# A two-layer hybrid encoder on one core: TensorE's small steps pinned in emission order, and two attention stages that hand over twice as often

## The chip, the cores and the metric

One core of one Trainium2 chip runs the whole program. The time is device microseconds from launch to end; the kernel before was run three times (2702.85, 2710.77 and 2712.8 us, median 2710.77 us), and once more with the profiler. The engines are named as in the profile: PE is TensorE's matmuls, PEld its weight loads, DVE is VectorE, ACT ScalarE, POOL GpSimd, SP the engine that issues the DMAs.

## The reference

The model is an encoder of two layers on a sequence of 1024 tokens with 1024 features, in float32. What matters of it:

```python
h = rms_norm(x, norm1_g[l])
proj = h @ w_in[l]                       # columns for four head groups
y_a = mla_mixer(...)    # A: 4 heads, full softmax over 1024 keys, latent q, k, v
y_b = diff_mixer(...)   # B: 4 heads, each softmax(q0 k0) - lam * softmax(q1 k1), then rms_norm of the head
y_c = swa_mixer(...)    # C: 4 heads, a band of +-128 keys and a sink
y_d = na_mixer(...)     # D: 4 heads, a 2-D neighbourhood with a learnt bias
mix = concatenate([rms_norm(y_a), y_b, rms_norm(y_c), rms_norm(y_d)])
x = x + mix @ w_out[l]
x = x + square(relu(rms_norm(x, norm2_g[l]) @ w_up[l])) @ w_down[l]
```

After the second layer comes a last rms_norm.

## The kernel before

Everything is kept transposed, features on the partitions and tokens along the free axis. A float32 product is made of three passes over operands split into a rounded high part and a low remainder: high by high, high by low, low by high (`passes`, L222 to L224). A pass is one matmul of 128x512. Splitting a weight block takes an ACT copy (L196) and a subtraction on POOL (L190).

A layer runs through these stages. First, projections of the columns for B, with every bank of PSUM. Then four attention stages, B, D, C and A, each as the *main* stream of a helper `weave`, with projections as its *fill*: in B the fill is three latent projections for A and the six for D; in D the four for C and A's products from the latent (`mm<-latp`); in C and A the early part of the output projection (`mm<-mix...`). Then the rest of the output projection, and the MLP, whose TensorE order is written out by hand.

In B and A (`dense`) the main stream goes by groups of 256 queries: for each 128 queries scores on PE (`sb<-stack`, two matmuls of 128x512 for each softmax in B, six in A), the minimum on DVE (L812), the exponential on ACT (L815); B makes two softmaxes for each 128 queries and combines them on ACT (L898) and POOL. The tiles of the group before are meanwhile transposed on PE (`tr<-ident,p`), split on ACT (`pth<-tr`) and DVE (`ptl<-tr`), and multiplied with the values (`pv<-pth`, `pv<-ptl`). In D and C (`banded`) it goes by 128 keys, and the scores are 128x256 or 128x384.

Beside main and fill there are *tails*: a queue of small chains that finish what a head has begun. A chain of denominators (`denominators`) takes the reciprocal on DVE, transposes the 128x8 column on PE (`mm<-ident,rz`), copies it, stores it to DRAM and loads it back spread over the partitions. A chain of norms (`sub_norm`, `mix_group`) goes on: multiply on POOL, square on ACT, sum by a matmul with ones (`mm<-pairs,rz` or `mm<-ones,sq`), reciprocal root, transpose (`mm<-ident,rs_r`), store, spread, multiply, split (`mixh`, `mixl`). `tick` takes one step of the first chain.

`weave` takes one step of main at a time, and after each step `every` ticks (the numbers `EV`) and `ratio` steps of fill. What it fixes is the emission order. The order in which each engine gets its instructions is then found by a scheduler, which knows the dependencies, the tiles' buffers and a priority: the place in emission order, moved ahead by `lead` instructions for main (40 in B, 50 in D, 0 in C and A). Buffers bind it too: the projections, the transposed columns and the sums of the norms all take turns on two PSUM banks, `mm`. Every engine then works through its own instructions strictly in that order.

Of the kernel before, what the change touches and what calls it, by code (L numbers as in the profile page):

```python
# [144 lines left out]
    return t.rearrange("f h s -> (f h) s")  # L145


class Trunk:
    def __init__(self, ctx, tc, d, out):
        self.ctx, self.tc, self.nc, self.d, self.out = ctx, tc, tc.nc, d, out  # L150
        self.ahead, self.tails = 4, deque()
        pool = lambda **k: ctx.enter_context(tc.tile_pool(**k))
        self.const = pool(name="const", bufs=1)
        self.xp = pool(name="xp", bufs=8)
        self.big = pool(name="big", bufs=16)
        self.wp = pool(name="wp", bufs=3)
        self.cp = pool(name="cols", bufs=2)
        self.dram = pool(name="dram", bufs=1, space=bass.MemoryType.DRAM)
# [222 lines left out]
    def attention(self, l):  # L381
# [33 lines left out]
        def proj_c():  # L415
            tabs = self.table("64", rb, nc.gpsimd)
            for t in range(2):
                yield from one(T_CQ2[t], xs, self.ev_rope(tabs, qc[:, t]))
            yield from one(T_CK, xs, self.ev_rope(tabs, kc))
            yield from one(T_CV, xs, self.ev_plain(rb, self.to_values(vc)))  # L420
# [3 lines left out]
        with ExitStack() as stack, ExitStack() as att:  # L424
            self.ap = att.enter_context(sbuf("att"))
            with self.banks(mm=2, tr=2, sb=3, pv=1):
                with sbuf("proj", "right") as self.pp:
# [20 lines left out]
                    for t in range(2):  # L448
# [6 lines left out]
                        if t == 0:  # L455
# [5 lines left out]
                    self.weave(chain.from_iterable(self.attn_b(l, t, qb, kb, vb, y["b"]) for t in range(2)),  # L461
                               fill, self.RB, self.LB, every=self.EV[0])
                    self.tails.append(self.mix_b(mix, y["b"], self.gsub[:, l:l + 1]))
                    fill = chain(proj_c(), self.latent_up(l, lat, rows, qa, ka, va))
                    self.weave(self.attn_d(l, qd, kd, vd, y["d"]), fill, self.RD, self.LD, every=self.EV[1])
                gout = lambda n: self.gout[n][:, l]
# [5 lines left out]
                def groups_bd():  # L472

                    for m in range(self.EARLY):
                        x = wo.tile([P, S], F, tag="sum", bufs=self.EARLY, name="sum")
                        self.load(x, saved[m])
                        sums.append(x)
                    while None in mix[:4]:
                        yield True
                    for m, x in enumerate(sums):  # L480
                        ws = self.weights(w_out[m, 0])
                        for n in range(2):
                            ps = self.mm_ps()
                            self.product(ps, ws, mix[:4], n)
                            sl = slice(n * 512, n * 512 + 512)
                            self.tt(x[:, sl], ps, x[:, sl], ALU.add)
                            yield True

                fill = groups_bd()
                self.weave(self.attn_c(l, qc, kc, vc, y["c"]), fill, self.RC, end=False, every=self.EV[2])  # L490
                self.tails.append(self.mix_group(mix, 4, y["c"], gout("swa")))
                self.weave(self.attn_a(l, qa, ka, krd, va, y["a"]), fill, self.RA, self.LA, every=self.EV[3])
                self.tails.append(self.mix_group(mix, 6, y["a"], gout("mla"), nc.vector))
# [43 lines left out]
                        self.product(ps, ws, mix[4:], n)  # L537
                        add(x, ps, partial, n)

    EV = (.5, .5, .7, 1)  # L540
    EARLY, RC, RA, LA = 4, (8, 1), (3, 1), 0
    WAVES = [(T_BQ[t], T_BK[t], T_BV[t]) for t in range(2)]
    NP, RB, RD, LB, LD = 6, (7, 8), (3, 2), 40, 50

    def weave(self, main, fill=iter(()), ratio=(1, 0), lead=0, end=True, every=1):


        due, steps = ratio[1] if lead else 0, 0
        while True:
            with self.tc.high_priority(offset=lead):  # L550
                if next(main, None) is None:
                    break
            steps += every
            while steps >= 1:
                steps -= 1
                self.tick()
            due += ratio[1]
            while due >= ratio[0]:
                due -= ratio[0]
                next(fill, None)  # L560
        if end:
            for _ in fill:
                pass
# [207 lines left out]
        yield  # L771


    def tick(self):
        while self.tails:
            if next(self.tails[0], self) is not self:
                return
            self.tails.popleft()

    def drain(self):  # L780
        while self.tails:
            self.tick()
# [35 lines left out]
    def dense(self, heads):  # L818

        nc = self.nc
        ready = []

        def product(job, j, h, lo):
            probs, g, v, y, half, done = job
            if g % 2 == 0 and j == 0:
                self.pv = self.bank("pv")
            out = self.pv[:, (g % 2) * 256:(g % 2) * 256 + 256]  # L830
            for k in range(2):
                kt = j * 2 + k
                sl = slice(k * 256, k * 256 + 256)
                nc.tensor.matmul(out, v[:, kt], h[:, sl], start=kt == 0, stop=False)  # L834
                nc.tensor.matmul(out, v[:, kt], lo[:, sl], start=False, stop=kt == 7)  # L835
            if j == 3:
                if g % 2:
                    self.pv_out(self.pv, y, half, g // 2)
                if g == 3:
                    done()  # L840

        def step(job, j):
            t = self.bank("tr")
            for k in range(2):
                for i, p in enumerate(job[0]):
                    nc.tensor.transpose(t[:, k * 256 + i * P:k * 256 + (i + 1) * P],  # L846
                                        p[:, (j * 2 + k) * P:(j * 2 + k + 1) * P], self.ident)
            h, lo = self.transposed(512)
            self.split(h, lo, t)
            ready.append((job, j, h, lo))  # L850
            if len(ready) > 1:
                product(*ready.pop(0))

        job = None
        for head in heads:
            tile_probs, *rest = head()
            for g in range(4):
                probs = []
                for i in range(2):
                    probs.append(tile_probs(g * 2 + i))  # L860
                    if job:
                        step(job, 2 * i)
                        step(job, 2 * i + 1)
                job = (probs, g, *rest)
                yield True
        for j in range(4):
            step(job, j)
        product(*ready.pop(0))
        yield True
# [629 lines left out]
```

## Time and profile before

| what | value |
| --- | --- |
| median of three runs | 2710.77 us (2702.85 to 2712.8) |
| profiled execution, its span | 2709.95 us, 2707.9 us |
| PE busy, share of the span | 2549.6 us, 94% |
| DVE, ACT, POOL busy | 1943.0, 1439.8, 1130.9 us |
| layer 1: B, then D, then C | 83 to 330, to 406, to 480 us |
| layer 1: A, then the output projection | 480 to 635, to 699 us |
| layer 1: MLP | 699 to 1345 us |
| layer 2: B, then D, then C | 1420 to 1669, to 1749, to 1820 us |

The boundaries are the starts of the first scores of a stage on PE. The second layer repeats the first. A page's PE row counts a matmul from its start to a modelled end, so matmuls that follow each other closely overlap; how far apart they start is read from the timeline.

### The profile page before, as it was taken

Reading aid. Unit: us, or ns where it says so; the run is one execution under the profiler, and the core shown is the slowest. Engines: PE = TensorE matmul, PEld = TensorE weight load, DVE = VectorE, ACT = ScalarE, POOL = GpSimd, SP = SyncE. Lnnn points to the kernel's source line nnn. Section 1 sums busy time; section 2 is a strip of 40 time slices with the busy share of each in tenths; the row PEclk is TensorE's granted clock in tenths of the full one; section 3 lists DMA queues with packets and bytes.
Section 4 is the critical chain, followed back from the end, with each engine's and each line's share of the span. In section 5 each row is a group of like instructions: output and inputs, shape, how many; then the busy total and the mean of one; then the engine's idle time right before and its main releaser. Section 6 shows DMA issues by size and latency. Waiting matters only on the chain.

```text
span 2707.9 us, 37502 instructions
## 1 busy us (share of the span) xinstructions
PE 2549.6 (94%) x12296; PEld 2112.5 (78%) x12296; DVE 1943.0 (72%) x3379; ACT 1439.8 (53%) x2601; POOL 1130.9 (42%) x754
## 2 busy tenths in 40 slices
PE   8989988999899998999999999889998999999997
PEld 6778876787778887888877788668876788878886
DVE  6777866774966668887567777677749666688775
ACT  4667756664534444444436776566635344444444
POOL 2555642201345554545434656321013455544442
PEclk9989988999999999999998899899999999999998
DMA  5534597222144457444244446962221444664431
GB/s 175 169 107 129 158 287 239 82 89 63 46 144 148 153 170 267 143 142 141 95 139 134 121 113 183 295 202 69 71 71 52 154 153 152 221 221 146 136 105 63
DMA packets 186931, 389.19 MB, mean 144 GB/s; under 512 B 23712, under 2 KB 26736, under 8 KB 186736
## 3 DMA queue, kind: packets, MB, share of 16 engines
q1 hardware_dynamic: 172912, 361.62, 43.2%
q10 hardware_dynamic: 13824, 25.17, 2.7%
q8 instruction: 97, 1.59, 0.2%
q14 instruction: 98, 0.80, 0.1%
HBM read 263.29 MB, written 123.41 MB: 143 GB/s over the span
## 4 chain that ended last, share of the span: by engine, by line
PE 73%; DVE 12%; DMA 6%; ACT 4%; issue 3%; POOL 1%; SPq 0%; DVEq 0%; ACTq 0%; POOLq 0%
PE u L222 8%; PE u L224 8%; PE u L223 8%; PE mm L222 5%; PE mm L223 5%; PE mm L224 5%; PE p L222 5%; PE p L223 5%; PE p L224 5%; PE sb L810 3%; PE tr L846 3%; DVE p L812 2%; DVE part L190 2%; PE pv L835 2%; PE pv L834 2%
## 5 line engine op out<-in xcount | busy, mean ns | idle before, releaser
L190 POOL TENSOR_TENSOR wl<-raw,wh 128x512 fp32r<-128x512 f32 x448 | 632.8, 1413 | 704.8 <-ACT wh L196 691.0
L196 ACT ACTIVATE wh<-raw 128x512 fp32r<-128x512 f32 x448 | 281.5, 629 | 576.2 <-PE u L223 310.9
L190 POOL TENSOR_TENSOR wl<-ws,wh 128x512 fp32r<-128x512 f32 (+1 forms) x112 | 147.3, 1316 | 461.0 <-ACT wh L196 436.1
L222 PE MATMUL u<-far,wh 128*128 128x512 f32 x768 | 301.8, 393 | 11.4 <-ACT ev L1242 8.3
L224 PE MATMUL u<-far,wl 128*128 128x512 f32 x768 | 300.6, 391 | 2.2 <-POOL wl L190 2.2
L190 DVE TENSOR_TENSOR raw<-raw 128x512 f32<-128x512 f32 x256 | 223.1, 877 | 109.1 <-POOL wl L190 55.6
L223 PE MATMUL u<-far,wh 128*128 128x512 f32 x768 | 300.6, 391 | 0.0
L190 DVE TENSOR_TENSOR ptl<-tr,pth 128x512 fp32r<-128x512 f32 (+2 forms) x384 | 238.3, 629 | 68.5 <-ACT pth L196 66.8
L815 ACT ACTIVATE p<-p,nm 128x1024 f32<-128x1024 f32 x192 | 220.2, 1147 | 92.3 <-DVE nm L812 91.6
L196 ACT ACTIVATE pth<-tr 128x512 fp32r<-128x512 f32 (+2 forms) x384 | 205.2, 546 | 108.5 <-PE tr L846 64.9
L222 PE MATMUL p<-far,wh 128*128 128x512 f32 x640 | 252.9, 395 | 7.5 <-DVE ev L190 7.5
L224 PE MATMUL p<-far,wl 128*128 128x512 f32 x640 | 251.5, 393 | 1.5 <-POOL wl L190 1.5
L223 PE MATMUL p<-far,wh 128*128 128x512 f32 x640 | 252.2, 394 | 0.0
L810 PE MATMUL sb<-stack 96*128 96x512 f32 x640 | 217.5, 422 | 22.1 <-DVE nm L812 21.4
L190 DVE TENSOR_TENSOR far<-act,far 128x512 fp32r<-128x512 f32 x224 | 207.3, 955 | 14.7 <-ACT far L196 14.7
L190 POOL TENSOR_TENSOR p<-p 128x1024 f32<-128x1024 f32 x64 | 154.0, 2411 | 129.6 <-ACT p L898 121.3
L222 PEld LDWEIGHTS u<-far,wh 128*128 128x128 f32 x768 | 145.3, 189 | 43.5 <-ACT ev L1242 9.1
L222 PE MATMUL mm<-xh,wh 128*128 128x512 f32 x416 | 170.9, 411 | 0.8 <-DVE part L190 0.3
L224 PEld LDWEIGHTS u<-far,wl 128*128 128x128 f32 x768 | 145.2, 189 | 33.5 <-POOL wl L190 3.0
L812 DVE CUSTOM_DVE_ANT_0 p<-sb,zero,nm 128x512 f32<-128x512 f32 x192 | 142.4, 743 | 37.7 <-PE sb L810 34.6
L223 PEld LDWEIGHTS u<-far,wh 128*128 128x128 f32 x768 | 145.4, 189 | 30.0
L223 PE MATMUL mm<-xl,wh 128*128 128x512 f32 x416 | 167.7, 403 | 0.0
(245 smaller groups left out, 6110.1 us busy)
## 6 DMA issues: line engine op xcount, KB each, us to landing
act<-acts SPq DMA_DIRECT2D x224, 256.0 KB
raw<-in_w_up SPq DMA_DIRECT2D x128, 256.0 KB
acts<-ev SPq DMA_DIRECT2D x128, 256.0 KB
raw<-in_w_down SPq DMA_DIRECT2D x128, 256.0 KB
acts<-ev ACTq DMA_DIRECT2D x96, 256.0 KB
ws<-in_w_in SPq DMA_DIRECT2D x76, 256.0 KB
rz<-drows SPq DMA_DIRECT2D x40, 256.0 KB
stack<-kd SPq DMA_DIRECT2D x32, 256.0 KB
```

Source lines behind the costliest of these rows:

```text
L190: (eng or self.nc.vector).tensor_tensor(out=out, in0=a, in1=b, op=op)
L196: nc.scalar.activation(hi, src, AF.Copy)
L222: mm(ps, w[0], x[0][:, sl], start=start, stop=False)
L223: mm(ps, w[0], x[1][:, sl], start=False, stop=False)
L224: mm(ps, w[1], x[0][:, sl], start=False, stop=stop)
L810: self.nc.tensor.matmul(ps, q[:, qt * P:(qt + 1) * P], k[:, sl], start=i == 0, stop=i == len(passes) - 1)
L812: self.nc.vector.tensor_tensor_reduce(out=p[:, sl], in0=ps, in1=self.zero[:, 0:1].bitcast(F).broadcast_to([P, 512]), scale=-scale, scalar= ...
L815: self.nc.scalar.activation(p, p, AF.Exp, bias=nm[:, 1:2], scale=-1.0, accum_out=z)
L834: nc.tensor.matmul(out, v[:, kt], h[:, sl], start=kt == 0, stop=False)
L835: nc.tensor.matmul(out, v[:, kt], lo[:, sl], start=False, stop=kt == 7)
L846: nc.tensor.transpose(t[:, k * 256 + i * P:k * 256 + (i + 1) * P], p[:, (j * 2 + k) * P:(j * 2 + k + 1) * P], self.ident)
```

## The change

A wrapper `Kept` is put around TensorE. While a tick of `weave` runs, each TensorE instruction that it emits is tied behind the TensorE instruction emitted just before it. The scheduler may no longer move it ahead of that one; it may still move other work past it. Only TensorE's steps are tied: the DVE, ACT, POOL and DMA steps of the same chains are placed as before.

`dense` now yields after the first 128 queries of a group as well as after the second. B and A so have twice as many steps, and their ratios of fill are halved to match: `RB` from (7, 8) to (7, 4), `RA` from (3, 1) to (6, 1). `EV` for B goes from .5 to .3, so that B has 0.6 ticks where it had 0.5; for A it stays 1, so that A has two ticks where it had one. No instruction is added or removed.

```diff
+class Kept:
+    def __init__(self, trunk, engine):
+        self.trunk, self.engine = trunk, engine
+
+    def __getattr__(self, name):
+        f = getattr(self.engine, name)
+
+        def emit(*args, **kw):
+            ins = f(*args, **kw)
+            if self.trunk.kept and name != "dma_start":
+                self.trunk.tc.keep_in_program_order(ins)
+            return ins
+
+        return emit
+
 class Trunk:
+    KEPT = ("tensor",)
...
-        self.ctx, self.tc, self.nc, self.d, self.out = ctx, tc, tc.nc, d, out
+        self.ctx, self.tc, self.d, self.out = ctx, tc, d, out
+        engines = {e: getattr(tc.nc, e) for e in ("tensor", "vector", "scalar", "gpsimd", "sync")}
+        self.kept = False
+        self.nc = SimpleNamespace(**{n: Kept(self, e) if n in self.KEPT else e for n, e in engines.items()})
...
-    EV = (.5, .5, .7, 1)
-    EARLY, RC, RA, LA = 4, (8, 1), (3, 1), 0
+    EV = (.3, .5, .7, 1)
+    EARLY, RC, RA, LA = 4, (8, 1), (6, 1), 0
...
-    NP, RB, RD, LB, LD = 6, (7, 8), (3, 2), 40, 50
+    NP, RB, RD, LB, LD = 6, (7, 4), (3, 2), 40, 50
...
-                self.tick()
+                self.tick(True)
...
-    def tick(self):
+    def tick(self, kept=False):
+        self.kept = kept
         while self.tails:
             if next(self.tails[0], self) is not self:
-                return
+                break
             self.tails.popleft()
+        self.kept = False
...
                     if job:
                         step(job, 2 * i)
                         step(job, 2 * i + 1)
+                    if i == 0:
+                        yield True
```

What it does to the order is seen in three places. In the changed kernel every TensorE instruction is issued by the wrapper's line, so all of them read L158; ScalarE's lines are moved by 23 or more.

First, TensorE in stage B of the first layer, at the transposed denominators of the second head (`mm<-ident,rz`). `tr`, `pv` and `sb` are attention, `mm<-xh` and `mm<-xl` a projection. Before:

```order
L835 MATMUL pv<-ptl,v 128x256
L834 MATMUL pv<-pth,v 128x256
L810 MATMUL sb<-stack 128x512
L835 MATMUL pv<-ptl,v 128x256
L834 MATMUL pv<-pth,v 128x256
L835 MATMUL pv<-ptl,v 128x256
L846 MATMUL tr<-ident,p 128x128 x4
L810 MATMUL sb<-stack 128x512
L846 MATMUL tr<-ident,p 128x128 x4
L273 MATMUL mm<-ident,rz 8x128
L222 MATMUL mm<-xh_164,wh 128x512
```

Now:

```order
L158 MATMUL sb<-stack 128x512 x2
L158 MATMUL pv<-ptl,v 128x256
L158 MATMUL pv<-pth,v 128x256
L158 MATMUL pv<-ptl,v 128x256
L158 MATMUL pv<-pth,v 128x256
L158 MATMUL tr<-ident,p 128x128
L158 MATMUL sb<-stack 128x512 x2
L158 MATMUL pv<-ptl,v 128x256
L158 MATMUL pv<-pth,v 128x256
L158 MATMUL pv<-ptl,v 128x256
L158 MATMUL mm<-ident,rz 8x128
L158 MATMUL mm<-xh_164,wh 128x512
```

In both a projection begins right behind the transposes. Before, 66 of B's 128 scores and 240 projection matmuls stand ahead of them; now 79 scores and 192 projection matmuls, and the 89 instructions just ahead (16 of them scores) hold no projection at all.

Second, TensorE in D of the first layer, at the transposed denominators of B's third head (before, they come among B's last scores). Before, among the scores of D's first head:

```order
L223 MATMUL mm<-xl_193,wh 128x512
L982 MATMUL sb<-stack 128x384 x2
L224 MATMUL mm<-xh_192,wl 128x512
L846 MATMUL tr<-ident,p 128x128 x6
L834 MATMUL pv<-pth,v 128x256
L982 MATMUL sb<-stack 128x384 x2
L835 MATMUL pv<-ptl,v 128x256
L834 MATMUL pv<-pth,v 128x256
L835 MATMUL pv<-ptl,v 128x256
L982 MATMUL sb<-stack 128x384 x2
```

Now, at the end of the scores of D's second head:

```order
L158 MATMUL sb<-stack 128x384 x2
L158 MATMUL sb<-stack 128x256 x2
L158 MATMUL pv<-ptl,v 128x384
L158 MATMUL mm<-ident,rz 8x128
L158 MATMUL mm<-xh_164,wh 128x512
L158 MATMUL mm<-xl_165,wh 128x512
L158 MATMUL mm<-xh_164,wl 128x512
L158 MATMUL mm<-xh_168,wh 128x512
L158 MATMUL mm<-xl_169,wh 128x512
L158 MATMUL mm<-xh_168,wl 128x512
```

Now 72 projection matmuls stand between these scores and the next. Over the layer, 554 of the 624 projection matmuls stood ahead of D's first score, and now 414 do; ahead of D's second head it was 600, now 432, ahead of the third 624, now 552. Counted over B's TensorE order of the first layer, 18 of the 128 scores lay in stretches of 28 or more instructions with no projection among them, and now 52 do. In A, 96 early products of the output projection were done, now 84.

Third, ScalarE in stage B, at the square of the pair's output (`rz<-y`), which needs these same denominators after their way through DRAM and a multiplication on POOL. Before:

```order
L815 ACTIVATE p,z_2093<-p,nm 128x1024
L196 ACTIVATE pth<-tr 128x512
L196 ACTIVATE wh<-ws 128x512
L898 ACTIVATE p<-p,cb 128x1024
L916 ACTIVATE rz<-y 128x1024
L815 ACTIVATE p,z_2092<-p,nm 128x1024
L196 ACTIVATE wh<-ws 128x512
```

Now:

```order
L840 ACTIVATE p,z_2065<-p,nm 128x1024
L925 ACTIVATE p<-p,cb 128x1024
L219 ACTIVATE pth<-tr 128x512
L219 ACTIVATE wh<-ws 128x512
L943 ACTIVATE rz<-y 128x1024
L219 ACTIVATE pth<-tr 128x512
L219 ACTIVATE wh<-ws 128x512
```

The square stands behind 40 exponentials before and 39 now, that is behind scores 80 and 78, while the transposes moved from score 66 to score 79: the 14 scores between them are gone.

## The prediction

> **What bounds the kernel now.** I read the page's sums first, then the work of the engines by stage, then the groups of instructions of B, and last TensorE's timeline there. The page gives busy shares of the engines, and the shares of the chain of work that ended last:
>
> ```profile
> PE 2549.6 (94%) x12296; PEld 2112.5 (78%) x12296; DVE 1943.0 (72%) x3379; ACT 1439.8 (53%) x2601; POOL 1130.9 (42%) x754
> ...
> PE 73%; DVE 12%; DMA 6%; ACT 4%; issue 3%; POOL 1%; SPq 0%; DVEq 0%; ACTq 0%; POOLq 0%
> ```
>
> PE bounds the program as a whole. But the change touches only the attention stages, so the work by stage decides. Each row is a stretch of the first layer: B in two halves, D, C, A, the output projection. Columns are length, then each engine's busy time with its count, the granted PE clock, the DMA share and GB/s:
>
> ```profile
> 83.00:210.00 127.00, 114.41 (x575) 93.94 (x574) 99.81 (x240) 89.28 (x146) 72.69 (x41) 0.91 0.43 125
> 210.00:330.00 120.00, 119.69 (x661) 102.25 (x660) 91.68 (x235) 87.92 (x143) 70.22 (x42) 1.00 0.46 134
> 330.00:406.00 76.00, 66.70 (x362) 57.63 (x360) 47.25 (x126) 45.82 (x114) 35.75 (x23) 0.91 0.97 282
> 406.00:480.00 74.00, 61.06 (x309) 48.79 (x308) 52.01 (x139) 50.19 (x132) 17.05 (x10) 0.88 0.73 227
> 480.00:635.00 155.00, 146.74 (x899) 124.65 (x898) 113.86 (x255) 98.14 (x178) 15.95 (x10) 1.00 0.25 71
> 635.00:699.00 64.00, 64.00 (x291) 52.72 (x290) 34.55 (x47) 24.37 (x44) 16.66 (x14) 1.00 0.26 83
> ```
>
> The reader is to see two kinds of stretch. B's second half and the output projection have no PE idle at all (119.69 of 120, 64 of 64): there only PE's amount of work counts. B's first half, D and C leave 12.6, 9.3 and 12.9 us idle, and all three ran at a granted clock of 0.88 to 0.91. The change carries projections from B into D, so it carries PE work from the first kind into the second. Layer 2 has the same shape, so I work out one layer and double it:
>
> ```profile
> 1420.00:1545.00 125.00, 114.98 (x568) 94.21 (x567) 96.39 (x235) 85.88 (x141) 69.34 (x39) 0.89 0.43 121
> 1545.00:1669.00 124.00, 122.94 (x665) 104.07 (x664) 91.45 (x242) 92.60 (x149) 74.81 (x43) 0.99 0.46 132
> 1669.00:1749.00 80.00, 68.74 (x367) 59.61 (x366) 48.75 (x128) 47.38 (x117) 33.67 (x23) 0.89 0.99 288
> ```
>
> What a group of 256 queries of B costs each engine is in two views. First, PE's timeline (start, us, engine, line): starts are 0.12 us apart for `pv`, 0.69/7 = 0.10 for `tr`, 0.24 behind a score, 0.23 behind a projection.
>
> ```profile
> 178.12 0.28 PE L834 MATMUL pv<-pth,v 128*128 128x256 f32 x1
> 178.24 0.28 PE L835 MATMUL pv<-ptl,v 128*128 128x256 f32 x1
> 178.36 0.93 PE L846 MATMUL tr<-ident,p 128*128 128x128 f32 x7
> 179.05 0.48 PE L810 MATMUL sb<-stack 96*128 96x512 f32 x1
> ...
> 179.83 0.40 PE L810 MATMUL sb<-stack 96*128 96x512 f32 x1
> 180.07 0.40 PE L223 MATMUL mm<-xl,wh 128*128 128x512 f32 x1
> 180.30 0.40 PE L224 MATMUL mm<-xh,wl 128*128 128x512 f32 x1
> 180.53 0.39 PE L222 MATMUL mm<-xh,wh 128*128 128x512 f32 x1
> ```
>
> Second, the groups of instructions of B by form (busy us, mean ns of one, idle time before and what ended it):
>
> ```profile
> L815 ACT ACTIVATE p<-p,nm 128x1024 f32<-128x1024 f32 x63 | 72.2, 1147 | 28.8 <-DVE nm L812 28.4
> L812 DVE CUSTOM_DVE_ANT_0 p<-sb,zero,nm 128x512 f32<-128x512 f32 x63 | 46.7, 743 | 12.2 <-PE sb L810 10.8
> L812 DVE CUSTOM_DVE_ANT_0 p<-sb,zero 128x512 f32<-128x512 f32 x64 | 43.6, 686 | 12.8 <-PE sb L810 6.6 <-POOL p L190 4.5 <-PE tr L846 1.2
> L190 DVE TENSOR_TENSOR ptl<-tr,pth 128x512 fp32r<-128x512 f32 x56 | 37.8, 682 | 6.6 <-ACT pth L196 6.5
> L898 ACT ACTIVATE p<-p,cb 128x1024 f32<-128x1024 f32 x31 | 35.3, 1144 | 5.0 <-DVE cb L897 4.9
> L196 ACT ACTIVATE pth<-tr 128x512 fp32r<-128x512 f32 x57 | 32.5, 587 | 11.7 <-PE tr L846 11.3 <-PE pv L834 0.2
> L815 ACT ACTIVATION_READ_ACCUMULATOR p<-p,nm 128x1 f32 x63 | 11.8, 187 | 0.0
> L812 DVE DVE_READ_ACCUMULATOR2_ANT nm<- 128x1 f32 x127 | 10.4, 82 | 0.0
> L897 DVE TENSOR_SCALAR cb<-cb,z,nlam 128x1 f32<-128x1 f32 x31 | 8.4, 271 | 0.7
> L896 DVE RECIPROCAL cb<-z 128x1 f32<-128x1 f32 x31 | 4.9, 157 | 11.4 <-ACT p L815 11.4
> ```
>
> A group has 8 scores, 16 transposes and 16 `pv`: PE 8 x 0.24 + 16 x 0.10 + 16 x 0.12 = **5.4 us**. DVE has four minima pairs, two combinations and four splits: 4 x (0.743 + 0.686 + 2 x 0.082) + 2 x (0.271 + 0.157) + 4 x 0.682 = **10.0 us**. ACT: 4 x (1.147 + 0.187) + 2 x 1.144 + 4 x 0.587 = **10.0 us**. So where a group of B has projections among it (some 20 matmuls, 4.6 us), the three engines are even. Where it has none, DVE and ACT set the pace and PE idles 10.0 - 5.4 = 4.6 us.
>
> **The change part by part.** No instruction comes or goes on any engine, DMA issues included; so the whole effect is order.
>
> *(a) B without projections.* Counted in the order, 18 of B's 128 scores lay in stretches of at least 28 PE instructions without a projection; now it is 52. That is 34 scores, 4 1/4 groups, more. At 4.6 us each PE loses 4 1/4 x 4.6 = **+20 us**. Bounds: 0, if DVE and ACT work off these groups' backlog while PE runs the projections that stand before and behind them (DVE's whole sum in B, 99.81 + 91.68 = 191 us of 247, leaves room for that); and 31, if PE's idling also brings the lower clock: the row of B's first half ran at 0.91, worth 127 x 0.09 = 11 us. I take 20: buffers for scores and probabilities reach over a group or so, and the new stretches are 15, 16, 8, 7 and 6 scores long.
> [...]
>
> *(b) D with projections.* 140 of the 624 projection matmuls (140 x 0.23 = 32 us of PE work) leave B for D, where two bursts of 48 and 72 stand between scores. B gets shorter by their 32 us and D longer, except for what they fill. What D can give back is its idle 76 - 66.7 = 9.3 us, and the clock, 76 x 0.09 = 6.8: 16 us. I take **-14**, bounds 0 and -16. For it: the bursts need no attention data, so PE has something to do in D's first heads. Against: D's DMA share was 0.97, and the work carried over brings its own weight blocks and stores into D.
>
> *(c) Mix products.* A's fill does 84 instead of 96 early products of the output projection; 12 x 0.23 = 2.8 us fall behind A, where PE has no idle (64 of 64). A itself had 155 - 146.74 = 8.3 us idle and gets that much shorter only if PE bound it there. Bounds 0 and 2.8; **+1**, since PE was busy for most of A.
>
> *(d) The chains.* A step that comes too early makes an in-order engine wait. Two chains as they ran, from the transposed denominators to the next square:
>
> ```profile
> 432.16 0.38 PE L273 MATMUL mm<-ident,rz 128*8 128x128 f32 x2
> 450.27 2.34 POOL L190 TENSOR_TENSOR y<-y,rz 128x1024 f32<-128x1024 f32 x1 [8.31 <-DMA rz<-drows]
> 452.64 1.06 ACT L364 ACTIVATE sq<-y 128x1024 f32<-128x1024 f32 x1 [2.48 <-POOL y L190]
> ...
> 635.31 0.27 PE L273 MATMUL mm<-ident,rz 128*8 128x128 f32 x1
> 642.68 1.06 ACT L364 ACTIVATE sq<-y 128x1024 f32<-128x1024 f32 x1 [2.48 <-DVE y L190]
> ```
>
> It takes 7.4 us at the least (635.31 to 642.68) and 20.5 with a busy DMA (432.16 to 452.64). In B's second head the transposes now stand at score 79 and ACT's square still behind score 78, so ACT reaches the square before the denominators are out. Behind it on ACT stand the copies of `tr`, a weight copy and the next exponentials; DVE's splits and PE's `pv` wait for these. The cover is the burst of 48 projections that follows on PE, 48 x 0.23 = 11 us: enough for 7.4, short by 9.5 for 20.5. On the gain's side stands the longest wait of PE for a chain, in the view of waits over the span:
>
> ```profile
> PE mm L265 <- DVE sq L190: 4.1, 2, 3.8
> ```
>
> Tied steps could free PE of these 4 us. Bounds -4 and +9; B's DMA share is 0.43 to 0.46, so the chain there should be nearer to 7.4: **+1**.
>
> The sum is 20 - 14 + 1 + 1 = +8 a layer, **+16 us** for two. Against the profiled execution, 2709.95 us (span 2707.9, and 2 around it), that is 2726. The profiled one lies 0.8 below the median, 2710.77, so no correction is made.
>
> **The rivals.**
>
> *B only gets shorter.* If the stretches without projections cost nothing (a at 0), B loses its 32 us and D takes them into its holes: -14 to -16, +1, and 0 for the chains, about -13 a layer: **2684**. For it: B's second half is bound by PE, 119.69 of 120, and DVE's 191 us still fit into 247 - 32 = 215. Against it: DVE would then need 89% over all of B, and in the row of B's first half it stood at 79% while PE idled 12.6 us, so the two already collide at less.
>
> *They cancel.* (a) at 13 to 14, since half of a stretch's lag is made up in the burst behind it: **2710**. Nothing in the rows tells 13 from 20.
>
> *The square holds ACT.* If the chain in B takes 20 us instead of 7, each of some four heads a layer (B's four) leaves ACT, and PE behind it, uncovered by up to 9.5; at half of that, 4 x 5 x 2 = 40 us: **2750** (2710 + 40, with a and b cancelling). It decides from the point where the chain is longer than the 11 us of projections behind the transposes. For: the margin went from 14 scores to -1. Against: DMA share 0.46 there.
>
> *The change doesn't do what it says* is answered by the order: the steps have moved by dozens of places.
>
> **How the numbers follow.** The forecast's own case has 0.38, of which 0.30 above +0.5% (13.6 us, about what can be told from no change here) and 0.08 below it; the rival on the faster side 0.27; cancelling 0.20, and 0.03 that nothing is felt; ACT held 0.12. Slower 0.30 + 0.12 = 0.42, same 0.08 + 0.20 + 0.03 = 0.31, faster 0.27. The likeliest case by itself spans 2712 (a at 13) to 2742 (a at 28). The bounds of all terms, 0 - 16 + 0 - 4 = -20 and 31 + 0 + 2.8 + 9 = +43 a layer, give 2670 to 2796; that both ends meet in all terms is unlikely. 2680 to 2760 takes in all the cases named and leaves out 0.08 below, since a faster case may also win from the chains, and 0.06 above.
>
> **What would show it.** (a): in the profile after, B's DVE and ACT shares rise in the stretches without projections while PE idles there, in sum 20 us a layer more; PE's waits for `nm` (scores' buffers) grow. If B's PE idle stays at some 13 us, (a) is wrong. (b): D's row shows PE over 95% busy, a clock near 1.00 and 76 + 32 - 14 = 94 us; if D has over 100 us, DMA or the chains keep it. B with its 32 us less and 20 more should take 235 us. (c): the output projection's stretch, 64 us, grows by 1 to 3. (d): the square of B's second head comes less than 10 us behind its transposes, and PE shows no wait over 4 us for it; a stall of ACT of 8 us or more for POOL's product in several heads would put the last rival in place. The prediction as a whole fails if B is 15 us shorter than before in each layer.

## The result

The changed kernel takes 2789.73 us (median of four runs, 2785.83 to 2792.23) against 2711.11 us before: a ratio of 1.0295, with a 95% interval of 1.0271 to 1.0319. It is slower, as forecast, but by 79 us and not by 16; the time lies outside the range. The profiled execution has a span of 2790.4 us, 82.5 more than before.

First the work by stage, layer 1 of the changed kernel: B, D, the first head of C, the rest of C, and A from its first score to its last. Columns are length, busy time and count of PE, PEld, DVE, ACT and POOL, the granted PE clock, the DMA share and GB/s.

```profile
84.30:320.30 236.00, 215.75 (x1083) 173.67 (x1082) 180.05 (x459) 171.15 (x277) 125.09 (x67) 0.91 0.39 113
320.30:419.30 99.00, 94.55 (x512) 80.10 (x511) 57.20 (x140) 50.86 (x123) 43.65 (x31) 0.98 0.79 221
419.30:457.70 38.40, 18.94 (x81) 15.17 (x81) 16.91 (x39) 16.52 (x40) 9.91 (x7) 0.69 0.93 271
457.70:508.80 51.10, 39.97 (x214) 31.25 (x213) 34.14 (x98) 34.43 (x92) 11.03 (x7) 0.93 0.63 189
508.80:656.70 147.90, 135.18 (x790) 114.06 (x788) 105.74 (x237) 88.97 (x161) 18.23 (x10) 0.95 0.29 79
```

The same view of the kernel before, cut at the same scores (D stands in the prediction):

```profile
83.10:330.00 246.90, 234.00 (x1233) 196.13 (x1232) 191.39 (x474) 177.11 (x288) 142.81 (x82) 0.95 0.44 129
...
406.00:424.10 18.10, 14.97 (x87) 11.87 (x87) 14.72 (x37) 13.16 (x36) 1.29 (x1) 1.00 1.03 335
424.10:480.10 56.00, 46.19 (x225) 36.96 (x223) 37.38 (x103) 37.13 (x98) 15.76 (x9) 0.85 0.63 192
480.10:614.50 134.40, 128.54 (x785) 109.81 (x784) 102.49 (x234) 88.20 (x161) 15.95 (x10) 1.00 0.28 82
```

Two stages do what the order promised: B is shorter by 10.9 us, D longer by 23.0. Two others do what no term of the sum held: C's first head takes 38.4 us instead of 18.1, with PE busy for half of it at a clock of 0.69, and A takes 147.9 instead of 134.4 with nearly the same matmuls (790 and 785).

For all runs below I use one measure. **PE time lost** in a stage is its length less the time its matmuls would take at their undisturbed distance from start to start (for each shape the lower quartile in the kernel before). It holds idle time and the time lost to a lower clock: in the changed kernel a 128x512 matmul of a projection starts 0.42 us behind the one before at a granted clock of 0.50 (221.51 to 221.93) and 0.23 at 1.00 (223.08 to 223.31). In us, layer 1 / layer 2:

| kernel | ratio (95%) | B | D | C, first head | C, rest | A |
| --- | --- | --- | --- | --- | --- | --- |
| before | 1 | 30.5 / 33.1 | 19.6 / 22.7 | 5.9 / 3.6 | 24.3 / 23.0 | 14.6 / 14.0 |
| the change | 1.0295 (1.0271, 1.0319) | 52.3 / 49.0 | 10.3 / 17.6 | 26.3 / 20.2 | 22.5 / 21.5 | 27.1 / 26.0 |
| hand_only | 1.0072 (1.0056, 1.0088) | 35.1 / 30.0 | 19.6 / 20.7 | 15.0 / 12.6 | 22.1 / 23.8 | 13.0 / 14.0 |
| kept_only | 1.0357 (1.0339, 1.0374) | 45.7 / 44.9 | 24.1 / 28.1 | 19.8 / 21.4 | 22.5 / 25.1 | 25.3 / 22.7 |
| ties_b | 1.0142 (1.0116, 1.0168) | 53.0 / 43.7 | 10.0 / 15.4 | 22.0 / 23.7 | 19.5 / 20.3 | 12.9 / 12.9 |
| ties_ca | 1.0189 (1.0174, 1.0204) | 35.2 / 34.0 | 18.4 / 16.8 | 15.5 / 16.1 | 23.4 / 24.6 | 25.2 / 28.3 |
| ties_a | 1.0120 (1.0103, 1.0137) | 38.3 / 31.3 | 17.2 / 17.3 | 16.4 / 11.8 | 22.0 / 24.0 | 19.9 / 23.3 |
| tail_bank | 1.0261 (1.0232, 1.0290) | 30.3 / 24.6 | 31.9 / 36.8 | 7.0 / 14.2 | 30.2 / 28.9 | 24.5 / 25.3 |
| tail_bank_before | 1.0250 (1.0231, 1.0269) | 27.2 / 26.9 | 37.4 / 36.5 | 16.3 / 13.0 | 23.5 / 26.1 | 25.1 / 26.4 |
| more_ticks | 1.0163 (1.0145, 1.0181) | 44.7 / 39.2 | 18.6 / 20.8 | 4.3 / 8.4 | 14.5 / 12.4 | 31.4 / 34.0 |
| late_chain | 1.0027 (1.0014, 1.0040) | 30.7 / 28.3 | 18.7 / 16.7 | 13.7 / 18.4 | 21.9 / 20.4 | 13.3 / 12.7 |
| hand_same_ticks | 1.0088 (1.0061, 1.0116) | 30.9 / 30.5 | 22.5 / 21.8 | 14.8 / 13.4 | 21.7 / 19.9 | 12.7 / 14.1 |
| ticks_all | 1.0225 (1.0204, 1.0245) | 47.5 / 39.0 | 22.0 / 20.7 | 19.4 / 17.9 | 23.2 / 17.6 | 18.2 / 21.7 |
| before_more_ticks | 0.9939 (0.9920, 0.9958) | 33.5 / 31.2 | 15.2 / 16.9 | 6.0 / 7.0 | 18.3 / 19.4 | 15.8 / 13.3 |
| part4 | 1.0310 (1.0293, 1.0327) | 48.7 / 54.6 | 10.7 / 11.2 | 25.2 / 25.0 | 19.8 / 22.4 | 25.6 / 28.5 |

The change's row less the first row gives B +21.8 and +15.9, D -9.3 and -5.1, C's first head +20.4 and +16.6, the rest of C -1.8 and -1.5, A +12.5 and +12.0: 81.5 us for both layers, and the spans differ by 82.5. (The stages hold 2.8 us less work a layer, the 12 early products, which come back in the output projection.)

Where PE waits in C's first head, in the view of waits of PE from 419 to 458 us of the changed kernel (us in total, times, the longest):

```profile
PE sb L158 <- DVE nb L1116: 11.1, 1, 11.1
PE pv L158 <- DVE y L213: 7.7, 1, 7.7
```

Two waits make 18.8 of the 19.5 us of idle. What DVE, ACT and POOL were doing there, and when SP sent loads and stores (from the timelines of these engines; in brackets the idle time before and what ended it):

```profile
421.75 0.20 DVE L786 RECIPROCAL rz<-z 128x8 f32<-128x8 f32 x1 [1.13 <-ACT p L1088]
429.54 0.69 DVE L213 TENSOR_TENSOR part<-mm,rkv 128x512 f32<-128x512 f32 x1 [7.59 <-POOL both L213]
432.06 0.48 DVE L1116 CUSTOM_DVE_ANT_0 p<-sb,mask,nsink 128x256 f32<-128x256 f32 x1 [1.83 <-DMA mask<-in_swa]
...
440.04 1.41 DVE L223 SCALAR_TENSOR_TENSOR mixl<-rz,g_sub,mixh 128x512 fp32r<-128x512 f32 x2 [3.56 <-ACT mixh L222]
444.44 0.68 DVE L213 TENSOR_TENSOR y<-pv,pvt 64x512 f32<-64x512 f32 x1 [2.99 <-DMA yb<-y]
...
425.48 0.63 ACT L219 ACTIVATE wh<-ws 128x512 fp32r<-128x512 f32 x1 [3.77 <-DMA ws<-in_w_out]
427.54 0.63 ACT L219 ACTIVATE both<-part 128x512 fp32r<-128x512 f32 x1 [1.43 <-DMA qar<-both]
439.28 1.34 ACT L222 ACTIVATE mixh<-rz,g_sub 128x512 fp32r<-128x512 f32 x2 [4.75 <-DMA rz<-yb]
...
437.41 2.34 POOL L213 TENSOR_TENSOR y<-y,rz 128x1024 f32<-128x1024 f32 x1 [6.33 <-DMA rz<-drows]
...
419.82 4.84 SPq L192 DMA_DIRECT2D qar<-both  x4
426.36 0.54 SPq L185 DMA_DIRECT2D mask<-in_swa  x1
430.04 0.58 SPq L185 DMA_DIRECT2D rz<-yb  x1
...
439.78 0.33 SPq L192 DMA_DIRECT2D yb<-y  x1
```

The second wait goes back to B's norm chains, which are late. SP sends the load `rz<-yb` for B's first pair of heads at 430.0; ACT's split `mixh` waits for it, DVE's `mixl` waits for `mixh`, and the sum `y<-pv` stands behind `mixl` in DVE's order. But `mixl` is done at 441.45, and `y<-pv` waits 2.99 us more, for the store `yb<-y`. This store ends the chain of B's last pair: POOL multiplies (`y<-y,rz`) only when its rows have come through DRAM, at 437.41, and SP sends the store at 439.78. D's second pair of heads writes its `y` into the buffer that B's last pair leaves with this store (`y` has two buffers, L813). PE's next values product needs the bank that `y<-pv` empties. The first wait ends with the mask's load, which SP sent behind four stores of latent products; ahead of it DVE stood for 7.6 us at a latent product's evacuation, whose buffer waits for POOL, ACT and those same stores.

### The profile page after: what moved, and what is told of

Same layout as the page of the kernel before. It is cut to its first block, busy times and chain, and to the rows that moved or that the text cites. A ratio compares the mean times of both kernels' runs of the same rounds, so it can differ in the third digit from the quotient of the medians.

```text
span 2790.4 us, 37545 instructions
## 1 busy us (share of the span) xinstructions
PE 2588.3 (93%) x12296; PEld 2128.3 (76%) x12296; DVE 1951.8 (70%) x3379; ACT 1444.9 (52%) x2601; POOL 1132.1 (41%) x754
## 4 chain that ended last, share of the span: by engine, by line
PE 70%; DVE 11%; DMA 8%; ACT 4%; issue 4%; POOL 2%; SPq 1%; DVEq 0%; ACTq 0%; POOLq 0%
PE u L158 23%; PE mm L158 17%; PE p L158 15%; PE sb L158 5%; PE pv L158 5%; PE tr L158 4%; PE q L158 3%; DVE p L837 2%; DVE part L213 2%; DMA rz<-drows 1%; DVE ptl L213 1%; ACT p L840 1%; DMA drows<-rows 1%; SPq L185 1%; ACT pth L219 1%
## 5 line engine op out<-in xcount | busy, mean ns | idle before, releaser
L158 PE MATMUL u<-far,wh 128*128 128x512 f32 x1536 | 477.3, 392 | 9.3 <-ACT ev L1269 5.9
L158 PE MATMUL p<-far,wh 128*128 128x512 f32 x1280 | 401.2, 395 | 7.6 <-DVE ev L213 7.6
L158 PEld LDWEIGHTS u<-far,wh 128*128 128x128 f32 x1536 | 289.6, 189 | 72.6 <-ACT ev L1269 7.3
L158 PE MATMUL sb<-stack 96*128 96x512 f32 (+2 forms) x896 | 291.8, 417 | 43.8 <-DVE nb L1116 23.0
L158 PE MATMUL u<-far,wl 128*128 128x512 f32 x768 | 300.2, 391 | 1.5 <-POOL wl L213 1.5
L158 PEld LDWEIGHTS p<-far,wh 128*128 128x128 f32 x1280 | 243.4, 191 | 60.3 <-DVE ev L213 8.4
L158 PE MATMUL p<-far,wl 128*128 128x512 f32 x640 | 251.7, 393 | 1.2 <-POOL wl L213 1.2
L158 PE MATMUL tr<-ident,p 128*128 128x128 f32 x1376 | 235.7, 283 | 9.8 <-POOL p L213 5.0
L158 PE MATMUL pv<-pth,v 128*128 128x256 f32 (+2 forms) x672 | 210.2, 323 | 27.6 <-ACT pth L219 19.7
L158 PEld LDWEIGHTS sb<-stack 96*128 96x128 f32 (+1 forms) x896 | 164.5, 201 | 85.1 <-DVE nm L837 38.6
L158 PE MATMUL pv<-ptl,v 128*128 128x256 f32 (+2 forms) x672 | 206.8, 324 | 14.9 <-DVE ptl L213 12.5
L158 PEld LDWEIGHTS tr<-ident,p 128*128 128x128 f32 x1376 | 172.9, 146 | 31.6 <-DVE ptl L213 6.7
L158 PE MATMUL mm<-xh,wh 128*128 128x512 f32 x416 | 171.2, 412 | 0.6 <-DVE part L213 0.5
```

Of the source, the lines that this page charges most:

```text
L158: ins = f(*args, **kw)
```

## The experiments

**The parts of the change, one by one.** The handover without the ties:

```diff
 class Trunk:
-    KEPT = ("tensor",)
+    KEPT = ()
```

> The handover every 128 queries without the ties (all of TensorE's steps free again, EV, RB and RA as in the change). In the order, 480 projection matmuls stand ahead of D's first score (554 before, 414 in the change), 552 ahead of D's second head (600, 432), 36 of B's scores lie in stretches without projections (18, 52). Theory 1 (the projections come late, and the stores and reloads of C's inputs then meet at C's start): a small part of the loss, C's first head 18 to 25 us instead of 38, whole time 2715 to 2735. Theory 2 (the ties themselves make TensorE wait, where they are): no tie, so no loss in C or A, 2705 to 2720 us.

Measured 1.0072, 2728.0 us against 2706.18: inside the range of Theory 1 and outside that of Theory 2. C's first head takes 25.7 and 25.1 us, just above Theory 1's 25. C and A have no tie and C's first head loses 15.0 and 12.6 us all the same, so Theory 2 (only ties make C wait) cannot hold for C. PE's own timeline of the change speaks against it too: ahead of all its tail steps from B's first score to A's last PE stood idle for 0.8 us in layer 1 and not at all in layer 2 (before: 7.0 and 1.5).

The ties without the handover (no yield inside a group, `RB` (7, 8), `RA` (3, 1), `EV` .5 in B):

> The ties without the double handover (EV .5, RB (7, 8), RA (3, 1), no yield after the first 128 queries). 432 projection matmuls ahead of D's first score and 432 ahead of its second head, 50 of B's scores in stretches without projections: as late as in the change. Both theories: most of the loss is here, 2770 to 2800 us; A, with one tick a group instead of two, tells whether its 13 us a layer come with the ties (147 us from first to last score) or with the ticks (134).

Measured 1.0357, 2803.7 us, 4 above the range and more than the whole change. The ties carry the loss, and the double handover with its ticks takes back some of it. A lost 25.3 and 22.7 us with one tick a group: its loss does not come from the number of ticks.

The ties in some stages only, by an argument of `weave`:

```diff
-    def weave(self, main, fill=iter(()), ratio=(1, 0), lead=0, end=True, every=1):
+    def weave(self, main, fill=iter(()), ratio=(1, 0), lead=0, end=True, every=1, kept=True):
...
-                self.tick(True)
+                self.tick(kept)
...
-                    self.weave(self.attn_d(l, qd, kd, vd, y["d"]), fill, self.RD, self.LD, every=self.EV[1])
+                    self.weave(self.attn_d(l, qd, kd, vd, y["d"]), fill, self.RD, self.LD, every=self.EV[1], kept=False)
```

> The change with the ties in B alone; D, C and A are woven without. Projections stay late (414 ahead of D's first score, 432 ahead of its second head, 590 ahead of its third), but no step of C or A is tied. Theory 1: C's first head stays long, 28 to 38 us; A is back at 133; whole time 2750 to 2765. Theory 2: C's first head is back at 18 to 20 us, whole time 2730 to 2740.

> The change with the ties in C and A alone. Projections as with the handover alone (480, 552, 600), TensorE's tail steps in C and A tied as in the change (no early product of the output projection ahead of A's first score, 84 at A's end). Theory 1: C's first head 18 to 25 us; if the ties lengthen A, 146 us there and 2740 to 2750 in all. Theory 2: C's first head 33 to 38 us, A 146, whole time 2770 to 2785.

> The change with the ties in A alone: 22 early products of the output projection stand ahead of A's first score (0 with C's ties too), 48 by A's middle. If A's 13 us a layer come from the ties in A (its transposed denominators 24 to 36 scores later): A 142 to 147 us, whole time 2740 to 2755. If they come from the products that C's ties hold back until A: A 130 to 135, whole time 2722 to 2732.

Against hand_only, ties in B cost 17.9 and 13.7 us in B, give back 9.6 and 5.3 in D, and add 7.0 and 11.1 in C's first head; A stays at 12.9. With ties in C and A it is B and C that stay, and A loses 25.2 and 28.3. With ties in A alone A loses 19.9 and 23.3: 7 to 9 us of A's loss come from A's own ties, 5 from C's, which push all early products of the output projection (22 in layer 1, 16 in layer 2) behind A's first score. A itself took 137.0 and 141.7 us with its own ties alone, between the two forecasts of that run. The whole time of ties_b (2748.83) lies 1 us below the range of Theory 1 and 9 above that of Theory 2; ties_ca (2758.62) lies 9 above the one and 11 below the other, so its time decides nothing. C's first head does: 33.5 and 35.2 us in ties_b, inside Theory 1's range, and 26.4 in ties_ca, 1 above it and 7 below Theory 2's. A by stage, ties_a ahead of hand_only:

```profile
494.60:631.60 137.00, 126.45 (x773) 107.03 (x772) 102.81 (x233) 86.85 (x159) 13.51 (x8) 1.00 0.28 77
```

```profile
492.50:622.50 130.00, 125.44 (x773) 107.03 (x772) 102.67 (x233) 87.64 (x159) 14.08 (x8) 1.00 0.29 83
```

Same 773 matmuls, same clock, 6 us more idle. In the changed kernel the largest wait of PE in A is for the split of the mix, in ties_a for the copies of the transposes; there ACT stood at a weight copy, whose weights had not landed (view of waits of PE, A alone, for each; and a row of ACT's timeline of ties_a). These waits are only a part: 4.1 of the 12.7 us that PE idles in A of the changed kernel, where its clock is 0.95 as well.

```profile
PE mm L158 <- ACT mixh L222: 4.1, 1, 4.1
```

```profile
PE pv L158 <- ACT pth L219: 3.3, 3, 2.2
...
574.79 0.42 ACT L219 ACTIVATE wah<-ws 128x256 fp32r<-128x256 f32 x1 [3.06 <-DMA ws<-in_w_out]
```

**Why ties hold projections back.** The tail steps and the projections take turns on the same two PSUM banks. If a tied step holds its turn, the projections emitted behind it cannot start either. So the ties were kept and the tail steps got other banks:

```diff
     def rstd_cols(self, sq, count, rhs, tag="mm"):
+        if self.kept: tag = "tr"
...
-        ps = self.bank("mm", [n, P])
+        ps = self.bank("tr" if self.kept else "mm", [n, P])
```

> The change with one thing altered: the tail steps' PSUM tiles (transposed columns, sums of the norms) take turns with the transposes of the probabilities, not with the projections. The ties stay. In the order 600 projection matmuls now stand ahead of D's first score (414 in the change, 554 before), all 624 ahead of D's second head, 20 of B's scores lie in stretches without projections (52, 18), 36 early products of the output projection stand ahead of A's first score (0, 22). Theory 1 (a tied tail step holds the projections' bank for itself, and all loss follows from the fill that stands behind it): the loss is gone, C's first head 18 to 22 us, A 130 to 136, whole time 2690 to 2720. Theory 2 (the tied steps make TensorE itself wait): 2750 to 2790 as in the change.

> The kernel before (no ties, one handover for 256 queries) with its tail steps on the transposes' banks, as the control of the run with this bank in the change: 586 projection matmuls ahead of D's first score, 22 of B's scores in stretches without projections, 13 early products ahead of A. Both theories: 2690 to 2720 us; what this run gains is the bank's part, and the difference from the change with that bank is what ties and handover are worth by themselves: by theory 1 within 15 us, by theory 2 the change is 40 us or more behind.

The time of tail_bank taken alone, 2776.04 us, is the one that Theory 2 gave; the order and the control decide against it. With the ties and this bank 600 projection matmuls stand ahead of D's first score instead of 414, and B's loss is back at 30.3 and 24.6. So the turns on the shared bank are how the ties hold projections back, as Theory 1 had it, and how B loses by them. Against the control with the same bank ties and handover cost nothing in the whole time (2776.04 and 2776.34 us). But both times miss the range of 2690 to 2720 by 56 us: in both D loses 32 to 37 us, the rest of C 24 to 30 and A 24 to 26. With such losses on both sides the equal times do not show that ties are free in C and A.

The early projections are not what costs D so much. In layer 2 of a kernel that comes below, hand_same_ticks, 599 and 624 projection matmuls stand ahead of D's first and second head, in the control 597 and 624; D loses 21.7 us in the one and 36.5 in the other (D of layer 2, the control ahead of hand_same_ticks):

```profile
1714.90:1804.30 89.40, 67.65 (x354) 56.06 (x352) 50.86 (x133) 48.12 (x117) 33.43 (x22) 0.85 0.95 280
```

```profile
1692.70:1759.50 66.80, 57.27 (x310) 47.95 (x308) 42.77 (x116) 40.32 (x105) 23.37 (x15) 0.90 0.96 280
```

This leaves the bank shared with the transposes, or the order of other work that follows from it; which of the two, and how, was not separated.

**Late projections or late chains.** After these runs C's first head was open: it is long wherever projections are late, but also in hand_only. B's ticks were raised in the change, with all its ties:

```diff
-    EV = (.3, .5, .7, 1)
+    EV = (.5, .5, .7, 1)
```

> The change with EV .5 in place of .3 in B: one tick a step and so a whole tick for every 128 queries on the average of two steps. Projections stay as late as in the change (408, 432, 552 ahead of D's first three heads), but B's last norms come earlier (their sums at score 164 instead of 182, before: 166). Theory 1a (C's start is held by the late projections alone): both waits of C's first head remain, 32 to 38 us, whole time 2775 to 2795. Theory 1b (the second wait, 6.7 to 7.7 us ahead of the first values product, comes from B's late norm chain): the second wait goes, C's first head 25 to 31 us, whole time 2755 to 2775.

The projections are as late as in the change, and C's first head loses 4.3 and 8.4 us. Both waits are gone, not just the second:

```profile
421.00:434.60 13.60, 11.37 (x68) 9.02 (x67) 11.83 (x32) 11.91 (x32) 4.00 (x4) 1.00 1.04 307
```

So Theory 1a, mine until then, falls. The rest of C and B gained too, D and A lost 3 to 8 us more each a layer, and the whole came to 2751.07 us, 4 below the range of Theory 1b. The counter-test is the kernel before with B's ticks slowed and nothing else, so that the projections stay early and the chain comes late:

```diff
-    EV = (.5, .5, .7, 1)
+    EV = (.4, .5, .7, 1)
```

> The kernel before with B's ticks slowed from .5 to .4 and nothing else. In the order the projections stay where they were (554 ahead of D's first score, 597 ahead of its second head, 624 ahead of its third), but the sums of B's last norms move from score 166 to 182 and their transposes from 166 to 192, as late as in the change. Theory 1b (the late norm chain of B stops ScalarE and VectorE at C's start): C's first head loses 12 to 25 us of TensorE's time where it lost 4 to 6, whole time 2725 to 2750. Theory 1a (the late projections do it): C's first head as before, 4 to 8 us lost, whole time 2700 to 2720.

C's first head loses 13.7 and 18.4 us instead of 5.9 and 3.6, as Theory 1b said. The whole time missed its range: 2714.54 us, ratio 1.0027, which lies in the range of Theory 1a. D, the rest of C and A each lose a little less than before, B too in layer 2, and give back most of it. So the late chain alone costs C's first head 7.8 and 14.8 us; the change, with late projections as well, 20.4 and 16.6. The handover with the ticks' old rate shows the same head start to end: B, D and A as before, only C's first head longer.

> The handover every 128 queries without ties, and with the ticks halved so that their rate for 256 queries is that of before (.25 in B, .5 in A). Projections as before (552, 583, 624 ahead of D's first three heads, 23 of B's scores without), B's last norms at score 182 (before 166). Theory 1b: C's first head loses 10 to 20 us, whole time 2720 to 2740. Theory 1a: as before, 2700 to 2720.

Measured 1.0088, 14.8 and 13.4 us in C's first head. In layer 2 the sums of B's last norms stand at score 168, hardly later than before, and its first head loses 13.4 all the same; what goes with the loss is the time at which the chain's rows are sent, more than its place in the order. The time at which SP sends B's last norm rows (`rz<-yb`, the first of two), against C's first score in layer 1, puts these runs in a row: more_ticks 35.2 us ahead (385.8, 421.0), loss 4.3 us; before_more_ticks 14.4 ahead (394.1, 408.5), 6.0; before 9.7 ahead (396.3, 406.0), 5.9; hand_only 2.7 ahead (408.4, 411.1), 15.0; ties_b 4.8 behind (424.0, 419.2), 22.0; late_chain 6.9 behind (413.0, 406.1), 13.7; the change 10.7 behind (430.0, 419.3), 26.3. The order is not strict, but the three that send it over 9 us ahead lose 4 to 6, and the others 14 to 26. Over all 15 kernels of the table and both layers it is as plain: the 7 first heads with the load sent over 9 us ahead lose 3.6 to 8.4 us, the other 23, where it is sent 4.3 us ahead at most, lose 11.8 to 26.3.

More ticks everywhere, on the change and on the kernel before:

```diff
-    EV = (.3, .5, .7, 1)
+    EV = (.4, .6, 1, 1)
```

> The change, ties and all, with ticks of (.4, .6, 1, 1) in B, D, C and A instead of (.3, .5, .7, 1). Projections as late as in the change (432, 456, 528 ahead of D's first three heads, 42 of B's scores without), but the norms come earlier: B's sums at score 172 (182), D's at 238 (250), and 20 early products of the output projection ahead of A (0). If the chains' place, not the ties as such, decides in C and A: C's first head 14 to 22 us, A 136 to 142, whole time 2735 to 2755. If the ties decide: C and A as in the change, 2775 or more.

```diff
-    EV = (.5, .5, .7, 1)
+    EV = (.6, .6, 1, 1.4)
```

> The kernel before with more ticks, (.6, .6, 1, 1.4) instead of (.5, .5, .7, 1). Projections a little later (525, 552, 624), 32 of B's scores without (18 to 21 before), B's last norms at score 164 (166), 14 early products ahead of A (22). By the terms measured so far B loses 8 us more a layer, D gives back 3 to 5, C and A stay: 2710 to 2725. Below 2700 it would beat the kernel before.

With the ties, ticks_all came to 2768.79 us, 14 above the first range and 6 below the second: A went down to 18.2 and 21.7, so 4 to 9 us of A hang on the place of the chains, but C's first head, 27.6 and 26.0 us long where 14 to 22 were forecast, still lost 19.4 and 17.9; B's sums stand at score 172 there and their transposes still at 182. Without ties, before_more_ticks beats both kernels: 2692.65 us, ratio 0.9939. Its gain is not in B (3 us more lost in layer 1, 2 less in layer 2) but in D and in the rest of C, 4 to 6 us each a layer. The forecast of 2710 to 2725 had let B lose 8 us more a layer for its scores without projections, and C stay.

**What ends the first wait.** One more buffer for the evacuated projections, in the change:

```diff
-        return self.pp.tile([P, 512], F, tag="part", bufs=3, name="part")
+        return self.pp.tile([P, 512], F, tag="part", bufs=4, name="part")
```

> The change with four buffers instead of three for the evacuated projections (`part`); TensorE's order from the end of B's first head on is that of the change. It tells what ends TensorE's first wait in C's first head (11.1 us in layer 1, 7.0 in layer 2), where VectorE's next instruction waited 7.6 us for such a buffer (rkv), and the load of the mask ended 1.8 us later. If the buffer is what is late: the first wait shrinks to 3 to 7 us, the second (7.7 and 6.7 us, held by B's norm chain) stays or takes it over, whole time 2775 to 2788. If what is late is everything that comes through DRAM there (the mask's load stands behind the same stores): the wait stays at 9 to 12, whole time 2786 to 2795.

PE's waits in C's first head of this run, and the rows of DVE for the buffer, for the mask and for the sum `y`:

```profile
PE pv L158 <- DVE y L213: 9.3, 1, 9.3
PE mm L158 <- DVE part L213: 7.9, 1, 7.9
```

```profile
427.10 0.69 DVE L213 TENSOR_TENSOR part<-mm,rkv 128x512 f32<-128x512 f32 x1 [6.74 <-POOL both L213]
430.38 0.48 DVE L1116 CUSTOM_DVE_ANT_0 p<-sb,mask,nsink 128x256 f32<-128x256 f32 x1 [2.58 <-DMA mask<-in_swa]
...
441.87 0.68 DVE L213 TENSOR_TENSOR y<-pv,pvt 64x512 f32<-64x512 f32 x1 [2.89 <-DMA yb<-y]
```

DVE waits 6.7 us for a buffer again, then for the mask, and at the end for the store that leaves B's buffer. PE's first wait is 7.9 us, between the two forecasts, and its second 9.3: 17.2 in place of 18.8. In layer 2 they are 7.4 and 10.1 in place of 7.0 and 6.7, and the whole time, 2790.58 us, is the same. A buffer more is filled and waits for the same stores; as these rows read, it is the way through DRAM that is late at this border. Which of those transfers would have to move first (the latent stores, the mask behind them, the norm rows) was not tried apart.

## Why the prediction was wrong, point by point

*What bounds the kernel*: right in sign for B and D: taking PE work out of the one and into the other cost B and filled D. I took C's 12.9 us of idle for a property of C and did not ask what keeps it from being more.

*(a) B without projections, +20*: the number held, and that was partly luck. B lost 21.8 and 15.9 us more, and its length, forecast as 235, was 236.0 and 232.6. But the 20 us were worked out as idle time behind DVE, and idle time grew by 7.4 us in layer 1 (246.90 - 234.00 = 12.9 to 236.00 - 215.75 = 20.3) and 6.4 in layer 2. The waits for `nm`, which were to grow, went from 8.2 to 10.1 us and from 8.5 to 8.4. The clock has at most 9 us of the rest in layer 1 (0.95 of 246.9 us before, 0.91 of 236.0 now) and 3 in layer 2; some 6 us a layer stand in neither. The upper bound had the clock, the +20 did not. A clock below 1.00 did come with short idles alone: in layer 2 of the changed kernel PE's longest idle in B is 2.40 us, ahead of a score at 1474.25, and B's clock is 0.92.

*(b) D with projections, -14*: right in sign, 9.3 and 5.1 instead. D took 99.0 and 106.4 us where I said 94. Layer 1's PE was 94.55 busy of 99, as forecast; layer 2 kept 7 us idle and a clock of 0.94.

*(c) the mix products, +1*: **wrong step**. The 12 matmuls did fall behind A, but A lost 12 us a layer. C's ties, which moved the products that had filled the end of C into A, cost A 5 us (ties_ca less ties_a), and A's own tied steps 7 to 9; the waits for the mix's split and for weights, of which rows stand above, are a part of it. I had priced the moved work and not the place it was moved to.

*(d) the chains, +1, between -4 and +9*: **the step that failed most**. The margin that I examined, the square of B's second head, did hold: it starts at 230.57, 10.1 us behind the transposes (I had said under 10), and waits for nothing:

```profile
220.44 0.42 PE L158 MATMUL mm<-ident,rz 128*8 128x128 f32 x1
230.57 1.05 ACT L943 ACTIVATE rz<-y 128x1024 f32<-128x1024 f32 x1
```

The gain that the term allowed for came as well: PE's wait of 3.8 us at a sum of squares is gone. But I priced one chain at one place. The sums of B's last norms stand at score 182 of the order where they stood at 166, and I left this out: from 182 the way through DRAM ends on the other side of D's end, where ACT and DVE wait for it, and D's last heads for the buffer that it holds. It is not that the DMA is busier there: its share in C's first head is 0.93 now and was 1.03. C's first head lost 20.4 and 16.6 us more, above the term's whole range; moved alone (late_chain), the chain costs 7.8 and 14.8 of it.

*The rivals.* The one on the slower side had the mechanism in part, ACT and DVE held in order behind a chain that is late through DRAM, at the wrong place: it was said of B's square and it came true for B's split at C's start; the buffer that B's last pair holds was in no term. The faster ones are out: B did lose time.

*The sum*: in place of +8 a layer, measured it is +21.8 - 9.3 + 12.5 + 18.6 (C) in layer 1, and +15.9 - 5.1 + 12.0 + 15.1 in layer 2. The two large terms were good to 9 us; the two small ones, which had C and A to cover, were too small by 25 to 29.

## What to carry to other kernels

When small steps are pinned in the order, ask first what they share with the work that flows past them: here it was a PSUM bank whose turns follow emission order, so that pinning 8-wide transposes held back 512-wide projections by the hundred. Follow every chain that moves to its last consumer, past the end of its stage, and look at what the engines at that place have to do and who waits for the buffers that the chain holds: a margin checked where a chain starts says nothing about where it ends. And moving the small steps to other banks has its own price: on the banks of the transposes the kernel without ties became 2.5% slower (tail_bank_before).

## What the runs showed of the hardware

In late_chain the clock fell in a stretch in which PE was half busy. Its PE has no idle time above 1.55 us in C's first head of layer 1, yet its clock falls, in four microseconds in which PE was 2.13 busy, and is 0.50 for the 12 us that follow, while PE is busy for 82 to 89% of the time (windows of 4 us):

```profile
406.00:410.00 4.00, 3.44 (x25) 2.91 (x23) 2.47 (x8) 3.13 (x8) 1.29 (x1) 1.00 0.86 203
410.00:414.00 4.00, 2.13 (x9) 1.40 (x9) 1.92 (x7) 1.15 (x4) 0.00 (x0) 0.84 1.06 314
414.00:418.00 4.00, 3.51 (x11) 2.18 (x9) 1.51 (x3) 1.48 (x5) 1.67 (x1) 0.50 1.00 334
418.00:422.00 4.00, 3.28 (x9) 2.21 (x9) 2.64 (x5) 1.66 (x3) 1.92 (x2) 0.50 1.03 315
422.00:426.00 4.00, 3.55 (x8) 2.72 (x9) 2.10 (x4) 0.60 (x1) 0.00 (x0) 0.50 0.89 345
426.00:430.00 4.00, 3.85 (x22) 2.97 (x21) 3.28 (x10) 2.88 (x6) 2.43 (x2) 0.95 0.65 194
430.00:434.00 4.00, 2.87 (x17) 1.83 (x15) 3.94 (x13) 3.95 (x11) 1.34 (x2) 1.00 0.85 276
```

The clock is 1.00 or 0.50 in these windows, but for the two between a 1.00 and a 0.50 (0.84 and 0.95). While it was 0.50 the matmuls of a projection started 0.42 us apart (423.05 and 423.47). It came back only after 12 us of work with short gaps (0.79 us the longest). The rows show when it fell and when it rose, and not why. Here, then, a stall's price was not its length alone: of the 13.7 us that late_chain lost there only 27.60 - 22.22 = 5.4 were idle; I estimate the mean clock of 0.75 in the row below at 27.60 x 0.25 = 6.9.

```profile
406.10:433.70 27.60, 22.22 (x94) 15.89 (x92) 17.45 (x42) 14.45 (x33) 8.65 (x6) 0.75 0.91 283
```
